# Two of layer 1's adaLN groups computed by VectorE in layer 0's second feed-forward product, TensorE summing over partitions only

## The chip, the cores and the metric

The kernel runs on one core of a Trainium2 chip. Its time is the device time of one launch in microseconds. The core has five engines with a queue each, which meet only through semaphores: TensorE (PE, matmuls; its weight loads are listed as PEld), VectorE (DVE), ScalarE (ACT), GpSimd (POOL) and SyncE (SP, which issues nearly all DMAs).

## The reference

One denoising step of a two-layer hybrid backbone with 512 latent tokens and 128 prompt tokens (640 columns together), D = 1024. What matters here is the modulation, its uses, and the feed-forward product in whose time the change computes it:

```python
def trunk_layer(x, cond, p, ...):
    mod = (jax.nn.silu(cond) @ p['w_ada'] + p['b_ada'])[:, None, :]
    sh1, sc1, gt1, sh2, sc2, gt2 = jnp.split(mod, 6, axis=-1)
    h = rmsnorm(x, p['g_pre_mix']) * (1.0 + sc1) + sh1
    ... = _split(h @ p['w_in'], IN_SIZES)          # gated DeltaNet, HGRN2 and attention mixers
    x = x + gt1 * rmsnorm(mix @ p['w_out'], p['g_post_mix'])
    h = rmsnorm(x, p['g_pre_ffn']) * (1.0 + sc2) + sh2
    ff_a, ff_b = jnp.split(h @ p['w_ffn_in'], 2, axis=-1)
    x = x + gt2 * rmsnorm((jax.nn.silu(ff_a) * ff_b) @ p['w_ffn_out'], p['g_post_ffn'])
```

There are two conditioning vectors (latent and prompt), so `mod` is a product of two rows of 1024 with a 1024 x 6144 matrix in each layer.

## The kernel before

All activations lie with features on partitions and tokens on columns, in two halves of 320 columns. A matrix product keeps fp32 precision with three matmuls of split numbers (high x high, high x low, low x high): a weight block arrives by DMA in a `raw` buffer (L592), ScalarE writes its high part `wh` (L582), VectorE the rest `wl` (L583), and TensorE multiplies (L606). The adaLN matrix is taken in unsplit fp32, by matmuls of only 32 rows of output (L276, `silu_c` is silu of the conditioning, `cst` and `onet` hold constants).

`w_ada` is stored as three groups per layer, each 8 blocks of 128 rows by 4 pieces of 512 columns, 256 KB per block and piece. Group 0 gives the shift and gain of the input norm, groups 1 and 2 ("2 and 3" if one counts from one) the rest. `ada` is a generator: each step issues one load and one matmul (L275, L276), four pieces going to four column quarters of the array; at the end of a group ScalarE copies the sum (L282), four transposes turn it onto partitions (L285), and VectorE adds the biases (L290). `GR` says which groups a layer computes for itself: groups 1 and 2, in its input stage, in `gdn` right after the raw part of the first gated DeltaNet pair (`fill(100)`). There they lie in program order among the w_in product and the DeltaNet's convolutions and chunk terms (L743, L787, L846). Group 0 of layer 1 is computed in layer 0's feed-forward stage, a few steps at a time.

Layer 0's second feed-forward product (`ffo`) multiplies 22 blocks of activations, `fs`, each a high and a low part, with w_ffo. The first four output tiles take both halves at once; then tiles 4 to 7 of the first half, then those of the second. A finished tile is copied from PSUM by ScalarE (L1449) into a block `ys`, and its square is added to a statistic by ScalarE (L389) and VectorE (L391). The last `fs` blocks are split (L583) just before the product.

The order of instructions on each engine is fixed when the kernel is built: a scheduler goes by priorities (weights first), by free buffers and by the code's order. SBUF blocks come in tags: `h` (8 blocks), `r` (12), `w0` and `w1` (7 each); PSUM tags have two buffers each. An engine runs its instructions in that order and stands still where one has to wait.

Of the kernel before, what the change touches and what calls it, by code (L numbers as in the profile page):

```python
# [12 lines left out]
ALU = mybir.AluOpType  # L13
AX = mybir.AxisListType

L = 2
D = 1024
KD = 8
# [14 lines left out]
def local(piece):  # L33
    a, b = HALVES[piece]
    return slice(a - BASE[piece], b - BASE[piece])
# [12 lines left out]
NSP, NFILL, NPACE = 6, 8, 8  # L48
AD0, AD1 = 7, 3
UTAGS = ("w1", "w1", "w1", "h", "h", "r", "r", "r")  # L50
SPRI = 5000
NKEEP = 6
GR = (1, 2), (1, 2)
MPRI = 8000
HPRI = 0
KPRI = 0
# [10 lines left out]
V_GPM, V_GOM, V_GPF, V_GOF, V_BADA = 0, 8, 16, 24, 32  # L67
# [97 lines left out]
class Builder:  # L165
# [40 lines left out]
    def setup(self):  # L206
# [52 lines left out]
            nc.vector.tensor_tensor(out=self.lb[:, l], in0=g[:, l], in1=g[:, 0], op=ALU.subtract)  # L259
        nc.vector.tensor_scalar(out=self.lb1, in0=self.lb, scalar1=-1.0, scalar2=1.0, op0=ALU.mult, op1=ALU.add)  # L260

    def ada(self, l, groups, tag, btag, depth):
        nc, I = self.nc, self.I
        ring = [self.blk([128, 2, 512], tag=btag) for _ in range(depth)]
        unit = 0
        if l not in self.mods:
            self.mods[l] = self.small("mods", [128, 48, 2], bufs=2)
        mods = self.mods[l]
        for ng in groups:
            acc = self.ps(tag=tag)  # L270
            for k in range(KD):
                for j in range(4):
                    raw = ring[unit // 2 % depth][:, unit % 2]
                    unit += 1
                    nc.sync.dma_start(out=raw, in_=I["w_ada"][l, ng, k, j])  # L275
                    nc.tensor.matmul(acc[32 * j:32 * j + 32, :], lhsT=self.sc[:, k, :], rhs=raw,  # L276
                                     start=(k == 0), stop=(k == KD - 1), tile_position=(0, 32 * j))
                    if j % 2 or k + 1 < KD:
                        yield
            row = ring[unit // 2 % depth][:, unit % 2]  # L280
            unit += 1
            nc.scalar.activation(row, acc, AF.Copy)  # L282
            tp = self.ps(tag=tag)
            for b in range(4):
                nc.tensor.transpose(tp[:, b * 128:(b + 1) * 128], row[:, b * 128:(b + 1) * 128], self.ident)  # L285
            tpv = tp.rearrange("p (b j r) -> p b j r", b=4, j=4)
            for b in range(4):
                mv = mods[:, ng * 16:(ng + 1) * 16].rearrange("p (j b) s -> p j b s", b=4)[:, :, b]
                bv = self.vec[:, l, V_BADA + ng * 16:V_BADA + (ng + 1) * 16].rearrange("p (j b) -> p j b", b=4)[:, :, b]
                nc.vector.tensor_tensor(out=mv, in0=tpv[:, b, :, 0:2],  # L290
                                        in1=bv.unsqueeze(2).to_broadcast([128, 4, 2]), op=ALU.add)
            self.ada_end(l, ng)
# [1028 lines left out]
    def layer(self, l, h):  # L1321
        nc, I = self.nc, self.I
# [7 lines left out]
                for n in pre:  # L1330
                    self.gemm_acc(pre[n], I["w_in"][l, n], hv, KD, k0)
        inp = lambda n, halves=(0, 1): pre.pop(n) if n in pre else self.gemm(I["w_in"][l, n], hv, KD, halves)
        filler = self.ada(l, GR[l], "c1", "w1", AD0)
        fill = lambda n: [next(filler, None) for _ in range(n)]
        rb = lambda shape: self.blk(shape, tag="r")
        r2 = rb([128, 2, NT])
# [62 lines left out]
        for s in range(2):  # L1399
            tag, bt = f"c{s}", ("w1", "r")[s]  # L1400
# [11 lines left out]
            h2[s] = self.norm_quads(ts, sx, m["G2"], m["sh2"], s, tag, bt)  # L1412
        fs = [self.blk([128, 2, NT], F32R, "w0") for n in range(NSP)]
        ffi = lambda n, halves: self.gemm(I["w_ffi"][l, n], lambda e, k, s: h2[s][k // 4][e][:, k % 4], KD, halves)
        filler = self.ada(l + 1, tuple(g for g in range(3) if g not in GR[l + 1]), "c0", "r", AD1) if l + 1 < L else iter(())
        for halves in ((0,), (1,)):
            for n in range(NSP):
                pa = ffi(2 * n, halves)
# [6 lines left out]
        last, us = None, []  # L1425
# [7 lines left out]
        last()  # L1433
        fill(100)
        self.retable()
        for u, tag in zip(us, ["w0"] * (7 - NSP) + ["r"] * 4 + ["w1"] * 7 + ["r"] * 4):
            fs.append(self.blk([128, 2, NT], F32R, tag))
            self.split(fs[-1][:, 0], fs[-1][:, 1], u)
        ys = [self.wide("r") for s in range(2)]
# [3 lines left out]
        hn, xs = [None, None], {}  # L1443
        for pieces, ns in (((0, 1), range(4)),) + tuple(((q,), range(4, KD)) for q in (0, 1)):
            for n in ns:
                ps = ffo(n, pieces)
                for q in pieces:
                    s, sl = min(q, 1), local(q)
                    nc.scalar.activation(ys[s](n)[:, sl], ps[q], AF.Copy)  # L1449
                    self.stat_add(sy[s], ys[s](n)[:, sl], n, sl)  # L1450
            if len(pieces) == 2:
                continue
            q = pieces[0]
            s = min(q, 1)
            tag, bt = f"c{s}", ("h", "w0")[s]
            if s not in xs:
                xs[s] = self.x_load(self.xd[2 * l], s, bt)
            ts, x = xs[s]
            if nl is None:
                self.post_norm(x, ys[s], sy[s], m["P2"], q, tag)  # L1460
                a, b = HALVES[q]
                for g in range(2):
                    nc.sync.dma_start(out=self.O["yT"][:, 4 * g:4 * g + 4, a:b], in_=ts[g][:, :, local(q)])
            else:
                sx = self.stat(bt)
                self.post_norm(x, ys[s], sy[s], m["P2"], q, tag, sx)
                self.x_store(self.xd[2 * l + 1], s, ts)
                hn[s] = self.norm_mod(x, sx, nl["G1"], nl["sh1"], s, tag)
# [110 lines left out]
```

## Time and profile before

| | us |
|---|---|
| median of 3 runs | 2006.32 (2006.19 to 2007.88) |
| the profiled execution | 2005.87 |
| span of the profiled execution | 2004.1 |
| TensorE busy in it | 1938.8 |
| VectorE busy | 1296.2 |
| ScalarE busy | 1001.2 |

The profile covers one execution. Its span goes from the first to the last instruction, 1.8 us less than that execution's own time. All times of rows are from the start of the span. A busy time is the union of an engine's instructions; "x4" is a count of records, and a row of a timeline that has a count merges neighbours of one kind. For a matmul the profile writes two records to each fp32 matmul.

### The profile page before, as it was taken

What the parts mean: (1) busy time and instruction counts of PE and PEld (TensorE: products, weight loads), DVE (VectorE), ACT (ScalarE), POOL (GpSimd) and SP (SyncE); (2) the same over time, 40 slices, a digit from 0 to 9 for tenths busy, and PEclk for the clock granted to TensorE, in tenths of its full rate; (3) what the DMA queues carried; (4) which work ended last, traced back from release to release, by engine and by line L of the source; (5) the groups of instructions that cost most, each with busy time, mean ns of one, the idle gap of its engine ahead of it and who ended that gap; (6) DMA issues with size and microseconds to landing.
All of it is one profiled execution on the core that took longest, in us unless ns stands there. A gap on an engine that the chain in (4) does not pass through costs nothing. (4 is left out here: it accounts for less than half of the span.)

```text
span 2004.1 us, 39984 instructions
## 1 busy us (share of the span) xinstructions
PE 1938.8 (97%) x15696; PEld 1724.3 (86%) x15696; DVE 1296.2 (65%) x2834; ACT 1001.2 (50%) x2088; POOL 16.4 (1%) x64
## 2 busy tenths in 40 slices
PE   5999999999999999999999999999999999999997
PEld 2747888888999979999997497888899999999996
DVE  5627567685588657762586386678756977777245
ACT  3514253754676435552465251547457855555243
POOL 0000000000000000000000000000000000000000
PEclk9999999999999999999999999999999999999998
DMA  8643211110554452232585532112016542223344
GB/s 300 205 163 89 59 47 32 58 32 3 188 181 152 137 165 85 89 114 79 155 271 163 184 97 57 31 40 59 5 59 210 163 123 89 87 88 88 101 137 140
DMA packets 157997, 226.57 MB, mean 113 GB/s; under 512 B 39280, under 2 KB 66032, under 8 KB 157808
## 3 DMA queue, kind: packets, MB, share of 16 engines
q1 hardware_dynamic: 157168, 222.70, 36.1%
q8 instruction: 123, 2.02, 0.4%
q0 software_dynamic: 640, 1.31, 0.3%
q14 instruction: 66, 0.54, 0.1%
HBM read 209.99 MB, written 12.65 MB: 111 GB/s over the span
## 5 line engine op out<-in xcount | busy, mean ns | idle before, releaser
L582 ACT ACTIVATE wh<-raw 128x512 fp32r<-128x512 f32 (+2 forms) x634 | 391.4, 617 | 591.9 <-PE g L606 410.1
L583 DVE TENSOR_TENSOR wl<-raw,wh 128x512 fp32r<-128x512 f32 (+1 forms) x610 | 408.8, 672 | 376.0 <-ACT wh L582 336.0
L606 PE MATMUL g<-h,wh 128*128 128x320 f32 x2448 | 541.3, 318 | 1.6 <-DVE su L1297 0.7
L606 PEld LDWEIGHTS g<-h,wh 128*128 128x128 f32 x2448 | 397.4, 188 | 50.2 <-issue 28.8
L606 PE MATMUL g<-h,wl 128*128 128x320 f32 x1224 | 337.1, 316 | 0.5 <-DVE wl L583 0.5
L606 PE MATMUL g<-w,wh 128*128 128x320 f32 x1152 | 242.5, 311 | 5.5 <-ACT r L1405 5.5
L606 PEld LDWEIGHTS g<-h,wl 128*128 128x128 f32 x1224 | 215.9, 188 | 21.4 <-issue 15.6
L606 PEld LDWEIGHTS g<-w,wh 128*128 128x128 f32 x1152 | 188.8, 189 | 6.3 <-ACT r L1405 6.0
L606 PE MATMUL g<-r,wh 128*128 128x320 f32 x768 | 162.9, 310 | 0.0
L606 PE MATMUL g<-w,wl 128*128 128x320 f32 x480 | 131.0, 310 | 0.0
L513 PE MATMUL g<-h,wh 128*128 128x320 f32 x768 | 129.1, 310 | 0.0
L606 PEld LDWEIGHTS g<-r,wh 128*128 128x128 f32 x768 | 125.9, 188 | 0.5
L513 PEld LDWEIGHTS g<-h,wh 128*128 128x128 f32 x768 | 116.3, 188 | 3.6 <-issue 3.4
L507 DVE TENSOR_TENSOR raw<-raw,raw 128x512 f32<-128x512 f32 x128 | 88.0, 688 | 2.2
L606 PEld LDWEIGHTS g<-w,wl 128*128 128x128 f32 x480 | 86.0, 189 | 0.2
L513 PE MATMUL g<-w,wh 128*128 128x320 f32 x512 | 85.9, 310 | 0.0
L513 PE MATMUL g<-r,wh 128*128 128x320 f32 x512 | 85.5, 309 | 0.0
L276 PE MATMUL m<-w,silu_c 128*32 128x512 f32 x256 | 83.4, 603 | 0.2 <-DMA w<-in_w_ada_dram 0.2
L513 PEld LDWEIGHTS g<-w,wh 128*128 128x128 f32 x512 | 77.6, 188 | 3.4 <-ACT r L525 3.4
L606 PE MATMUL g<-r,wl 128*128 128x320 f32 x288 | 78.6, 309 | 0.0
L513 PEld LDWEIGHTS g<-r,wh 128*128 128x128 f32 x512 | 77.7, 188 | 0.0
L513 PE MATMUL g<-h,wl 128*128 128x320 f32 x384 | 71.9, 309 | 0.0
(373 smaller groups left out, 3030.2 us busy)
## 6 DMA issues: line engine op xcount, KB each, us to landing
raw<-in_w_ffi_dram SPq DMA_DIRECT2D x224, 256.0 KB
w<-in_w_ada_dram SPq DMA_DIRECT2D x160, 256.0 KB
raw<-in_w_ffo_dram SPq DMA_DIRECT2D x120, 256.0 KB
raw<-in_w_in_dram SPq DMA_DIRECT2D x106, 256.0 KB
raw<-in_w_out_dram SPq DMA_DIRECT2D x64, 256.0 KB
r<-in_w_ada_dram SPq DMA_DIRECT2D x32, 256.0 KB
r<-in_xT_dram SPq DMA_DIRECT2D x6, 640.0 KB
xd<-w SPq DMA_DIRECT2D x6, 640.0 KB
```

Of the source, the lines that this page charges most:

```text
L276: nc.tensor.matmul(acc[32 * j:32 * j + 32, :], lhsT=self.sc[:, k, :], rhs=raw, start=(k == 0), stop=(k == KD - 1), tile_position=(0, 32 * j))
L507: nc.vector.tensor_tensor(out=o, in0=a, in1=b, op=ALU.add)
L513: nc.tensor.matmul(ps, lhsT=w[e][:, k], rhs=a[f][:, k], start=first and i == 0, stop=i == 11, skip_group_check=not first)
L582: self.nc.scalar.activation(hi, src, AF.Copy)
L583: self.nc.vector.tensor_tensor(out=lo, in0=src, in1=hi.bitcast(F32), op=ALU.subtract)
L606: self.nc.tensor.matmul(ps[h], lhsT=w[:, k], rhs=rhs(e, kk, h), start=(kk == 0 and i == 0), stop=(kk == nk - 1 and i == 2))
```

## The change

Layer 1 no longer computes groups 1 and 2 for itself (`GR[1]` is empty). A new generator, `ada_vec`, does it in layer 0's second feed-forward product. A unit is one piece of 512 columns of one group, and there are eight. VectorE multiplies each of the eight 128x512 blocks with the conditioning (one number per partition) and adds them up in `acc`, for both conditionings: 2 `tensor_scalar_mul` and 14 `scalar_tensor_tensor`. Then TensorE sums over the partitions: eight matmuls with a single column of ones (`onet`), into one PSUM tile, and VectorE adds the biases. The loads are 512 KB each, four to a unit, into a ring of two blocks of tag `r`; `acc` is a third. Two units are placed ahead of each of the first four output tiles. To make room for a block, the last `fs` block moves from tag `r` to `h`. Group 0 of layer 1 is computed where it was.

```diff
-GR = (1, 2), (1, 2)
+GR = ((1, 2), ())
+PE_NEXT, VEC_NEXT = (0,), (1, 2)
+VRING = 2
...
+    def ada_vec(self, l, groups, tag, btag):
+        nc, I = self.nc, self.I
+        mods = self.modulation(l)
+        acc = self.blk([128, 2, 512], tag=btag)
+        ring = [self.blk([128, 2, 512], tag=btag) for _ in range(VRING)]
+        for ng in groups:
+            for j in range(4):
+                for k in range(KD):
+                    raw = ring[k // 2 % VRING]
+                    if k % 2 == 0:
+                        nc.sync.dma_start(out=raw, in_=I["w_ada"][l, ng, k:k + 2, j].rearrange("k p n -> p k n"))
+                    for s in range(2):
+                        c = self.sc[:, k, s:s + 1]
+                        if k == 0:
+                            nc.vector.tensor_scalar_mul(acc[:, s], raw[:, 0], c)
+                        else:
+                            nc.vector.scalar_tensor_tensor(out=acc[:, s], in0=raw[:, k % 2], scalar=c, in1=acc[:, s],
+                                                           op0=ALU.mult, op1=ALU.add)
+                tp = self.ps((128, 4, 2), tag)
+                for s in range(2):
+                    for b in range(4):
+                        nc.tensor.matmul(tp[:, b, s:s + 1], lhsT=acc[:, s, b * 128:(b + 1) * 128], rhs=self.onet, start=True, stop=True)
+                q = ng * 16 + j * 4
+                bv = self.vec[:, l, V_BADA + q:V_BADA + q + 4]
+                nc.vector.tensor_tensor(out=mods[:, q:q + 4], in0=tp, in1=bv.unsqueeze(2).to_broadcast([128, 4, 2]), op=ALU.add)
+                yield
+            self.ada_end(l, ng)
...
-        filler = self.ada(l, GR[l], "c1", "w1", AD0)
+        filler = self.ada(l, GR[l], "c1", "w1", AD0) if GR[l] else iter(())
...
-        filler = self.ada(l + 1, tuple(g for g in range(3) if g not in GR[l + 1]), "c0", "r", AD1) if l + 1 < L else iter(())
+        filler = self.ada(l + 1, PE_NEXT, "c0", "r", AD1) if l + 1 < L else iter(())
...
-        for u, tag in zip(us, ["w0"] * (7 - NSP) + ["r"] * 4 + ["w1"] * 7 + ["r"] * 4):
+        filler = self.ada_vec(l + 1, VEC_NEXT, "c0", "r") if l + 1 < L else iter(())
+        for u, tag in zip(us, ["w0"] * (7 - NSP) + ["r"] * 4 + ["w1"] * 7 + ["r"] * 3 + ["h"]):
...
         for pieces, ns in (((0, 1), range(4)),) + tuple(((q,), range(4, KD)) for q in (0, 1)):
             for n in ns:
+                if len(pieces) == 2:
+                    fill(2)
                 ps = ffo(n, pieces)
...
             if len(pieces) == 2:
+                fill(100)
                 continue
```

In the changed program lines have moved: L582, L583, L606 and L1449 are L615, L616, L639 and L1485. A row names a line, an operation, the block written and those read, with numbers that tell blocks apart; `r_9622` is `acc`, `r_9623` and `r_9624` are the ring, `m` and `g` are PSUM tiles, and the brackets name what the instruction waits for.

VectorE at the start of the second feed-forward product, in the changed program. Ahead is the last split of the activations; in the program before, only weight splits and statistics follow it.

```order
L616 TENSOR_TENSOR h_9613<-r_9272,h_9613 128x640 [waits DVE_49]
L283 TENSOR_SCALAR r_9622<-r_9623,silu_c 128x512 [waits DMAHW5_49]
L283 TENSOR_SCALAR r_9622<-r_9623,silu_c 128x512
L285 SCALAR_TENSOR_TENSOR r_9622<-r_9623,silu_c,r_9622 128x512 [waits DVE_49] x2
L616 TENSOR_TENSOR wl_9839<-raw_9837,wh_9838 128x256 [waits DMAHW0_49,PE_49,Activation_49]
L688 TENSOR_SCALAR ga_n_11912<-ga_n_11912 128x4
L285 SCALAR_TENSOR_TENSOR r_9622<-r_9624,silu_c,r_9622 128x512 [waits DMAHW0_49,DVE_49]
L285 SCALAR_TENSOR_TENSOR r_9622<-r_9624,silu_c,r_9622 128x512 [waits DVE_49] x3
L616 TENSOR_TENSOR wl_9923<-raw_9921,wh_9922 128x512 [waits DMAHW1_49,PE_49,Activation_49]
```

Each block of the ring gives four operations on VectorE, and a weight split follows about every fourth of them; 112 rows of L285 and 16 of L283 stand in this stretch, with 34 weight splits between.

TensorE where the third one-half tile of the first half begins (tile 6), in the program before and then in the changed one.

```order
L606 MATMUL g_10430<-r_9613,wh_10522 128x320 x2
L606 MATMUL g_10430<-r_9613,wl_10523 128x320
L606 MATMUL g_10536<-w_886_6295,wh_10538 128x320 [waits Activation_49]
L606 MATMUL g_10536<-w_886_6295,wh_10538 128x320
L606 MATMUL g_10536<-w_886_6295,wl_10539 128x320 [waits DVE_49]
```

```order
L639 MATMUL g_10680<-h_9613,wl_10773 128x320
L290 MATMUL m_10353<-onet,r_9622 128x1 [waits DVE_49,PE_49]
L290 MATMUL m_10353<-onet,r_9622 128x1 x3
L290 MATMUL m_10353<-onet,r_9622 128x1 [waits DVE_49]
L290 MATMUL m_10353<-onet,r_9622 128x1 x3
L639 MATMUL g_10786<-w_886_6295,wh_10788 128x320 [waits Activation_49]
L639 MATMUL g_10786<-w_886_6295,wh_10788 128x320
L639 MATMUL g_10786<-w_886_6295,wl_10789 128x320
L639 MATMUL g_10786<-w_887_6296,wh_10788 128x320 x2
L639 MATMUL g_10786<-w_887_6296,wl_10789 128x320
L639 MATMUL g_10786<-w_888_6297,wh_10788 128x320 x2
L290 MATMUL m_10383<-onet,r_9622 128x1 [waits DVE_49,PE_49]
```

The narrow matmuls of unit 7 (`m_10353`) now stand at the end of tile 5, and those of unit 8 (`m_10383`) after the first eight matmuls of tile 6; the six units before stand earlier, spread over the tiles 0 to 5.

ScalarE at its copy of the first one-half tile (tile 4), before and then changed.

```order
L1449 ACTIVATE r_9617<-g_10324 128x320 [waits PE_49]
L389 ACTIVATE h_9620<-r_9617 128x320 [waits Activation_49]
L582 ACTIVATE wh_10486<-raw_10485 128x512 [waits DMAHW6_49,DVE_49,PE_49]
```

```order
L615 ACTIVATE wh_10824<-raw_10823 128x512 [waits DMAHW4_49,DVE_49,PE_49]
L1485 ACTIVATE r_9617<-g_10574 128x320 [waits DMAHW1_49,DVE_49]
L1485 ACTIVATE r_9617<-g_10680 128x320 [waits PE_49]
L422 ACTIVATE h_9620<-r_9617 128x320 [waits Activation_49] x2
L615 ACTIVATE wh_10842<-raw_10841 128x512 [waits DMAHW5_49,PE_49]
```

The copy waited for TensorE alone; now it waits for a load and for VectorE, since its target `r_9617` takes the place of a ring block, and it stands next to the copy of tile 5.

TensorE in layer 1's input stage, before and then changed, where the DeltaNet's triangular terms of the first pair begin.

```order
L606 MATMUL g_12707<-h_11309,wl_12740 128x320
L606 MATMUL g_12706<-h_10795,wh_12739 128x320
L276 MATMUL m_12089<-w_1840_12008,silu_c 32x512 [waits DMAHW1_49]
L606 MATMUL g_12707<-h_11309,wh_12739 128x320
L606 MATMUL g_12706<-h_10797,wh_12739 128x320
L787 MATMUL m_12230<-r_11687 64x128 [waits DVE_49,PE_49]
L787 MATMUL m_12230<-r_11687 64x128 x2
L276 MATMUL m_12089<-w_1840_12008,silu_c 32x512 [waits DMAHW2_49]
L787 MATMUL m_12230<-r_11687 64x128
```

```order
L639 MATMUL g_12870<-h_11558,wl_12873 128x320
L639 MATMUL g_12869<-h_11044,wh_12872 128x320
L820 MATMUL m_12290<-r_11937 64x128 [waits DVE_49,Activation_49]
L820 MATMUL m_12290<-r_11937 64x128 x7
L820 MATMUL m_12303<-r_11937 64x128 [waits Activation_49]
L820 MATMUL m_12303<-r_11937 64x128 x7
L639 MATMUL g_12870<-h_11558,wh_12872 128x320
```

The adaLN matmuls (L276) are gone from this stage, and w_in's matmuls (L606, now L639) stand next to the DeltaNet's (L787, now L820).

## Rows read from the trace of the kernel before

**Rows 1.** The page's table of engines: busy us, share of the span, instructions.

```profile
PE 1938.8 (97%) x15696; PEld 1724.3 (86%) x15696; DVE 1296.2 (65%) x2834; ACT 1001.2 (50%) x2088; POOL 16.4 (1%) x64
```

**Rows 2.** Stretches of 10 us, second feed-forward product: length, engines' busy us, clock, DMA.

```profile
core 0: us, PE busy (x) PEld busy (x) DVE busy (x) ACT busy (x) POOL busy (x), PEclk, DMA share, GB/s
...
880.00:890.00 10.00, 10.00 (x70) 10.00 (x69) 2.12 (x5) 1.68 (x3) 0.00 (x0) 1.00 0.24 67
890.00:900.00 10.00, 10.00 (x70) 10.00 (x69) 2.10 (x4) 2.91 (x6) 0.00 (x0) 1.00 0.66 213
...
940.00:950.00 10.00, 10.00 (x70) 10.00 (x69) 2.51 (x4) 2.88 (x7) 0.00 (x0) 1.00 0.27 73
950.00:960.00 10.00, 10.00 (x70) 10.00 (x69) 4.56 (x8) 4.52 (x9) 0.00 (x0) 1.00 0.46 129
```

**Rows 3.** Timeline of ScalarE: copies of finished tiles (start us, us, what).

```profile
949.04 0.75 ACT L1449 ACTIVATE r<-g 128x320 f32<-128x320 f32 x2
...
958.87 0.42 ACT L1449 ACTIVATE r<-g 128x320 f32<-128x320 f32 x1
...
968.55 0.42 ACT L1449 ACTIVATE r<-g 128x320 f32<-128x320 f32 x1
```

**Rows 4.** Timeline of VectorE: the last split of the activations.

```profile
879.42 0.82 DVE L583 TENSOR_TENSOR r<-r,r 128x640 fp32r<-128x640 f32 x1
```

**Rows 5.** Timeline of TensorE, layer 1's input stage.

```profile
1094.76 4.67 PE L276 MATMUL m<-w,silu_c 128*32 128x512 f32 x30
...
1101.03 2.03 PE L276 MATMUL m<-w,silu_c 128*32 128x512 f32 x4
...
1124.36 1.05 PE L276 MATMUL m<-w,silu_c 128*32 128x512 f32 x2
...
1153.24 1.05 PE L276 MATMUL m<-w,silu_c 128*32 128x512 f32 x2
...
1155.04 0.60 PE L285 MATMUL m<-cst,w 128*128 128x128 f32 x4
...
1167.65 1.24 PE L743 MATMUL m<-w,cst 128*128 128x512 f32 x4
```

**Rows 6.** Timeline of TensorE's weight loads around one adaLN group; brackets: idle before, releaser.

```profile
1124.36 0.14 PEld L276 LDWEIGHTS m<-w,silu_c 128*32 128x32 f32 x2 [0.19 <-issue]
1125.33 0.30 PEld L606 LDWEIGHTS g<-h,wh 128*128 128x128 f32 x2 [0.84 <-issue]
```

**Rows 7.** Stretches of 10 us from 1090 to 1170, and their sum.

```profile
1100.00:1110.00 10.00, 10.00 (x45) 4.74 (x43) 2.35 (x9) 4.40 (x11) 0.68 (x2) 1.00 1.00 370
...
1160.00:1170.00 10.00, 10.00 (x67) 9.52 (x66) 8.43 (x15) 4.00 (x10) 0.00 (x0) 1.00 0.36 96
sum 80.00, PE 80.00 PEld 46.45 DVE 38.54 ACT 26.60 POOL 2.26; mean PE 10.00 PEld 5.81 DVE 4.82 ACT 3.33 POOL 0.28
```

**Rows 8.** Two more stretches of 10 us, ahead of and behind those.

```profile
1020.00:1030.00 10.00, 10.00 (x69) 9.76 (x67) 6.82 (x13) 6.49 (x15) 0.34 (x6) 1.00 0.93 310
...
1170.00:1180.00 10.00, 9.88 (x60) 8.76 (x59) 9.72 (x28) 9.44 (x19) 0.00 (x0) 1.00 0.33 105
```

**Rows 9.** VectorE's instruction groups, shapes apart: busy us, mean ns, idle before.

```profile
L583 DVE TENSOR_TENSOR wl<-raw,wh 128x512 fp32r<-128x512 f32 x566 | 388.6, 688 | 337.9 <-ACT wh L582 298.2 <-PE g L606 16.3 <-PE g L513 11.1
L690 DVE SCALAR_TENSOR_TENSOR w<-w,vec,w 128x642 f32<-128x642 f32 x48 | 42.5, 885 | 1.1
...
L1243 DVE TENSOR_SCALAR h<-h,smax 128x640 f32<-128x640 f32 x32 | 17.6, 551 | 0.7
...
L575 DVE SCALAR_TENSOR_TENSOR r<-r,P,h 128x320 f32<-128x320 f32 x16 | 8.2, 545 | 1.7 <-ACT h L357 1.7
```

**Rows 10.** Timeline of VectorE: two neighbouring multiply-adds.

```profile
1001.53 1.01 DVE L575 SCALAR_TENSOR_TENSOR r<-r,P,h 128x320 f32<-128x320 f32 x2
```

**Rows 11.** Timeline of SyncE's queue and TensorE: an adaLN load and the matmul that waits.

```profile
708.43 0.33 SPq L275 DMA_DIRECT2D r<-in_w_ada_dram  x1
...
711.50 1.04 PE L276 MATMUL m<-r,silu_c 128*32 128x512 f32 x2 [0.29 <-DMA r<-in_w_ada_dram]
```

**Rows 12.** Stretches of 2 us around a wait of TensorE in layer 1's mixers.

```profile
1458.00:1460.00 2.00, 0.93 (x17) 0.60 (x12) 0.29 (x1) 0.60 (x1) 0.00 (x0) 0.97 0.00 0
1460.00:1462.00 2.00, 2.00 (x9) 1.75 (x10) 1.20 (x5) 1.28 (x5) 0.00 (x0) 0.50 0.00 0
1462.00:1464.00 2.00, 2.00 (x11) 1.79 (x10) 1.25 (x6) 1.49 (x5) 0.00 (x0) 0.67 0.03 8
```

More of the change, by code (lines that the diff above doesn't have):

```diff
@@ L260, in setup, with modulation @@
         nc.vector.tensor_scalar(out=self.lb1, in0=self.lb, scalar1=-1.0, scalar2=1.0, op0=ALU.mult, op1=ALU.add)
+    def modulation(self, l):
+        if l not in self.mods:
+            self.mods[l] = self.small("mods", [128, 48, 2], bufs=2)
+        return self.mods[l]
+    def ada_vec(self, l, groups, tag, btag):
[25 more added lines that the diff above has]
+            self.ada_end(l, ng)
     def ada(self, l, groups, tag, btag, depth):
@@ L265, in ada @@
         unit = 0
-        if l not in self.mods:
-            self.mods[l] = self.small("mods", [128, 48, 2], bufs=2)
-        mods = self.mods[l]
+        mods = self.modulation(l)
         for ng in groups:
```

## The prediction

> **What bounds the kernel now.** I read the page's table of engines first: TensorE is busy 97% of the span, the other engines far less [rows 1], so a microsecond taken from TensorE counts only where nothing else ends last, and one added to another engine counts only where TensorE then waits. So I read the two stages that the change touches, one after the other.
>
> *Where the work goes: layer 0's second feed-forward product.* The table by 10 us stretches shows TensorE full there, and VectorE at 2.1 to 2.5 of 10 us through the tiles that compute both halves, 4.6 of 10 after [rows 2]. ScalarE's copies of finished tiles give the pace: two-half tiles come out until 949.04, then one tile every 9.68 us (958.87, 968.55) [rows 3]; that is 66 matmuls (22 blocks of the inner dimension, 3 products) at 0.147 us. The window from VectorE's last split of the activations, 879.42 + 0.82 [rows 4], to the copy at 949.04 is 69 us long.
>
> *Where the work comes from: layer 1's input stage.* The timeline of TensorE shows a first block of adaLN matmuls of 4.67 us, then single groups of 1.04 to 1.05 us, strewn among the w_in product until 1153.24, and two groups of transposes of 0.60 us [rows 5]. Around one of them, the weight loads show that the next ordinary load starts 0.97 us after the group's own, which had itself waited 0.19 us [rows 6]: a group takes 1.16 us out of the stream.
>
> **Part 1, layer 1: what is removed.** In the timeline from 1094.76 to 1155.04 I count the block (4.60 us to the next matmul), one double group (1.95 + 0.19) and 25 single ones (25 x 1.16 = 29.0), and two transposes (1.2): 36.9 us. Six more groups lie at 1050.9 to 1063, where TensorE waits for the norm of the input anyway; I give them 0 to 1.5 us. So the gain is at most 38.4 us. What takes some of it back: once TensorE no longer fills the stage, VectorE and ScalarE must bring the same steps of the gated DeltaNet in less time. Between 1090 and 1170, VectorE is busy 38.54 and ScalarE 26.60 of 80 us, but VectorE is at 8.43 in the last 10 us of it [rows 7] and at 9.72 in the 10 us behind [rows 8]. With 36.9 us out, the 80 us shrink to 43, less room than VectorE has work unless it runs at 0.9 of busy. In 1020 to 1030, where splits and norms compete in the same way, it reached 6.82 of 10 [rows 8]. At that share 38.5 us of work takes 56 us: gain 24. I take 31, the middle of 24 and 38.4, since TensorE does have other w_in matmuls to run while the chain waits and VectorE's queue is not in every window that poor. The loads of these two groups (64 of 256 KB) leave a stretch whose DMA share reached 1.00 [rows 7]; that is inside the 0 to 1.5.
>
> **Part 2, layer 0: VectorE's added work.** Per unit of 512 columns of one group: 2 multiplications and 14 multiply-adds of 128x512, and there are 8 units: 16 and 112. The trace has no multiply-add of 128x512 with a scalar from a column; 128x320 takes 545 ns and 128x642 takes 885 [rows 9], so 128x512 lies at 746. A multiplication of 128x640 takes 551 [rows 9]; by its slope I take 484 for 512. Two neighbouring multiply-adds of 128x320 take 1.01 us together, not 1.09 [rows 10]: the next starts 0.08 early. So the pitches are 0.666 and 0.404, and the sum is 112 x 0.666 + 16 x 0.404 = 81.1 us (91.3 by full durations). Between them, in the order of the changed program, stand 28 splits of 128x512 (688 ns in [rows 9], pitch 0.61), 6 of 128x256, 4 additions of statistics and 8 of biases: 22.3 us (25.4 by durations). So VectorE's stretch is 103.4 us: begun at 880.2, it ends at 983.6 if it never waits, at 996.9 if nothing overlaps. **It does not fit into the 69 us.**
>
> It will wait, too. At each of the 7 changes of unit the first multiplication overwrites the sum that TensorE has still to read: some 1.3 us for signal, eight narrow matmuls and signal back, 9 us in all. And the ring has two blocks: a block is loaded again only when it has been used up. A 256 KB load of the same tensor took 3.07 us from issue to the matmul that waited for it [rows 11]; the other 256 KB of a 512 KB load add 0.7 us at the 370 GB/s of [rows 7], so 3.8. Meanwhile VectorE uses the other block up (4 x 0.666 = 2.7 us, and 0.7 of splits): it waits 0 to 0.4 us at each of 32 blocks, in the mean 0.3, or 10 us. End of the last unit: 983.6 + 9 + 10 = **1003** (993 without waiting for loads, 1015 at the upper ends).
>
> **Who waits for that.** TensorE runs in program order, and the narrow matmuls of the units stand in its row: five units among the two-half tiles, the sixth in the second one-half tile, the seventh at its end, the eighth after only 8 matmuls of the third. So the last two units are not covered: VectorE needs some 15 us for a unit (123 us for 8), and TensorE has only 48 matmuls (7 us) between the sixth and the seventh and 8 (1.2 us) between the seventh and the eighth. A second tie points the same way: the copy of the first one-half tile writes a block that the ring had, so ScalarE waits there for the last unit's third block, and the third one-half tile for ScalarE, since two PSUM buffers serve these tiles. In the trace of before, the eighth matmul of the third one-half tile starts at about 968.55 + 8 x 0.147 = 969.7 [rows 3]. Now it goes on at 1003 + 0.9 (the last four narrow matmuls): 34.2 us later; by the bounds 24 to 46. The 128 records of narrow matmuls, about 0.12 us each by four transposes in 0.60 us [rows 5], run inside that wait. After TensorE had stood still for half of a 2 us stretch, the granted clock in the next two stretches was 0.50 and 0.67 of full speed, so at the lower of its two levels (1.2 of 2.4 GHz) for a time [rows 12]; that cost 0.50 x 2 + 0.33 x 2 = 1.7 us there. Two waits here are longer: I add 2.5 us, 0 to 3.4 as bounds. Part 2: **+36.7**, from 24 to 49.
>
> **Sum.** 2005.87 (the profiled execution) + 36.7 - 31 = 2011.6; the median of the runs shown is 0.45 above the profiled one: **2012**.
>
> **Rivals.**
> *A, VectorE keeps up better (the other side).* Place: the second feed-forward product. If the ring's loads come in time and the changes of unit cost half of what I took, the last unit ends at 988 and TensorE loses 988 + 0.9 - 969.7 = 19, and if VectorE is no bound in layer 1, 37 comes back: 2005.9 + 19 + 1.7 - 37 = 1989; with one of the two only, 1996 to 2006. For it: the raw loads leave the queues at 0.24 to 0.66 share in this stretch [rows 2]. Against it: the 103.4 us hold no wait at all. It decides from an end of the last unit before about 996 at a full gain. Chance 0.22.
> *B, layer 1 gives back only 24,* because VectorE becomes the bound from 1130 on: 2005.9 + 36.7 - 24 = 2019. For it: 9.72 of 10 in [rows 8]. Against: TensorE has other tiles to run. Chance 0.15.
> *C, the ring is the bound:* a period of 3.8 us or more per block, since the issuing queue also holds weight loads that wait for their buffers in order. 32 x 0.8 us of waiting instead of 10 in all: end at 1018, +15: 2027. Chance 0.09.
> *D, nothing overlaps on VectorE:* each multiply-add waits by semaphore for the one two places ahead, on the same half of the sum. If that wait uses up the 0.08, the stretch ends at 996.9 + 9, and the loads are then hidden behind the longer steps: 1006, so 2005.9 + 36.2 + 2.5 - 31 = 2014, 2 us above the forecast. Against it: [rows 10], 1.01 us for two independent steps of 545 ns. Chance 0.04. The Trainium skill's page "VectorE: DVE Perf Modes", section "The DRAIN you can't avoid", says that the next VectorE operation does not start before the pipeline of the one ahead is empty, which speaks against chains of small steps like these; by that rule the durations would hold in full and D would be the case, and for independent steps [rows 10] do not agree with it.
>
> **How the numbers follow.** The forecast has the remaining 0.50, with a range of its own of 2003 to 2021 (end of the last unit 996 to 1009, gain 27 to 35). About 0.2% (4 us) is what a measurement of this kernel can tell from no change: 2002.3 and 2010.3 are the limits. Faster: A 0.20, the forecast's lower end 0.05: 0.25. Within: A 0.02, the forecast 0.16, B 0.02: 0.20. Slower: the rest, 0.55. Range for 8 in 10: at 1996 about 0.11 is left out below (the better part of A), at 2027 about 0.09 above.
>
> **What would show it.** Right: in the second feed-forward product VectorE near 9 of 10 us from 880 to about 1000; TensorE with waits for VectorE at the narrow matmuls of units 7 and 8 of about 5 to 20 us in all, or for ScalarE's copy ahead of the third one-half tile; this tile's copy about 35 us late; the granted clock down once or twice behind these waits. The distance from there to the L743 group of the second pair (1167.65 in [rows 5]) about 25 to 30 us shorter than before, and some 31 at the end of the stage. Wrong, if multiply-adds of 128x512 take much under 0.67 us apiece, if TensorE waits only a few microseconds there, or if VectorE is not full between 1090 and 1190 (shifted) and the stage shrinks by 37 all the same.

## The result, and the profile after

The changed kernel takes 2016.87 us (median of 4 runs, 2014.74 to 2022.63) where the kernel before, measured beside it, takes 2006.26. The ratio is 1.0056, with a 95% interval of 1.0044 to 1.0068: **11 us slower** (9 to 14). The forecast was 2012, in a range of 1996 to 2027.

The span of the profiled execution is 2020.8 us. It was the longest of the four, and some 4 us of that arose ahead of the changed place, as ScalarE's copies of finished tiles show. First those of the kernel before that [rows 3] leave out (the first tile, and tiles 6 and 7), then the same copies of the kernel after (start, us, what; in brackets the idle time before and who ended it).

```profile
890.96 0.75 ACT L1449 ACTIVATE r<-g 128x320 f32<-128x320 f32 x2
...
978.23 0.42 ACT L1449 ACTIVATE r<-g 128x320 f32<-128x320 f32 x1
987.90 0.42 ACT L1449 ACTIVATE r<-g 128x320 f32<-128x320 f32 x1
```

```profile
895.19 0.75 ACT L1485 ACTIVATE r<-g 128x320 f32<-128x320 f32 x2
922.28 0.75 ACT L1485 ACTIVATE r<-g 128x320 f32<-128x320 f32 x2
943.66 0.75 ACT L1485 ACTIVATE r<-g 128x320 f32<-128x320 f32 x2
967.76 0.75 ACT L1485 ACTIVATE r<-g 128x320 f32<-128x320 f32 x2
1010.20 0.77 ACT L1485 ACTIVATE r<-g 128x320 f32<-128x320 f32 x2 [20.25 <-DVE r L285]
1028.34 0.42 ACT L1485 ACTIVATE r<-g 128x320 f32<-128x320 f32 x1
```

The first tile is 4.2 us late. After it, tile by tile, the product falls behind: tile 3 by 19, and tile 6 by 50.1 (1028.34 against 978.23). So layer 0's product costs 46 us in this execution. Between tiles 3 and 4 ScalarE stands for 20.25 us and waits for VectorE: its next copy writes a block that the ring still holds.

The stretches of 10 us (columns as in [rows 2]) show the same on all engines.

```profile
880.00:890.00 10.00, 10.00 (x70) 10.00 (x69) 8.74 (x16) 2.58 (x6) 0.00 (x0) 1.00 0.60 194
...
900.00:910.00 10.00, 10.00 (x50) 10.00 (x50) 4.99 (x9) 1.26 (x2) 0.00 (x0) 0.67 0.69 233
...
950.00:960.00 10.00, 10.00 (x69) 10.00 (x70) 9.16 (x16) 1.69 (x3) 0.00 (x0) 1.00 0.61 203
...
990.00:1000.00 10.00, 1.52 (x8) 1.55 (x8) 6.87 (x12) 0.00 (x0) 0.00 (x0) 0.60 0.54 174
1000.00:1010.00 10.00, 2.02 (x10) 1.94 (x10) 7.60 (x13) 0.00 (x0) 0.00 (x0) 0.50 0.49 158
1010.00:1020.00 10.00, 9.31 (x38) 9.32 (x39) 4.56 (x10) 2.11 (x5) 0.00 (x0) 0.50 0.03 4
```

VectorE, at 2.1 to 2.5 of 10 in [rows 2], is now at 8 to 10 in most stretches. The exception is 900 to 910, with 4.99. There TensorE's granted clock was 0.50 from 900 to 906, behind a wait of 0.82 us at 897, so the mean of the ten microseconds is 0.67 and TensorE lost 3.3 us; in the middle of it VectorE stood 3.66 us for a weight split, whose first half ScalarE could write only when TensorE had freed a buffer:

```profile
907.63 0.63 ACT L615 ACTIVATE wh<-raw 128x512 fp32r<-128x512 f32 x1 [5.09 <-PE g L639]
908.30 0.69 DVE L616 TENSOR_TENSOR wl<-raw,wh 128x512 fp32r<-128x512 f32 x1 [3.66 <-ACT wh L615]
```

From 990 to 1010 TensorE works 1.5 to 2 us of each 10, and from 1010 to 1020 it works again, but at a granted clock of 0.50, its lower level (1.2 of 2.4 GHz). TensorE's timeline has the two waits that make this hole:

```profile
998.48 3.54 PE L290 MATMUL m<-onet,r 128*128 128x1 f32 x16 [9.06 <-DVE r L285]
1010.69 0.90 PE L639 MATMUL g<-w,wh 128*128 128x320 f32 x2 [8.66 <-ACT r L1485]
```

The first is unit 7's narrow matmuls waiting for VectorE, the second is tile 6 waiting for ScalarE's copy. VectorE's own waits from 884 to 1012 (us in total, times, longest) and its two new groups (busy us, mean ns):

```profile
DVE mods L293 <- PE m L290: 8.5, 7, 1.6
DVE r L285 <- DMA r<-in_w_ada_dram: 6.1, 7, 2.1
DVE wl L616 <- ACT wh L615: 5.2, 5, 3.7
DVE r L283 <- PE m L290: 3.0, 4, 1.4
...
L285 DVE SCALAR_TENSOR_TENSOR r<-r,silu_c,r 128x512 f32<-128x512 f32 x112 | 77.8, 746 | 6.1 <-DMA r<-in_w_ada_dram 6.1
L283 DVE TENSOR_SCALAR r<-r,silu_c 128x512 f32<-128x512 f32 x16 | 7.5, 482 | 3.0 <-PE m L290 3.0
```

In layer 1 the time comes back. The row that answers to L846 at 1205.08 in the timeline of before is L879 here, first before and then after:

```profile
1205.08 1.09 PE L846 MATMUL m<-w,w 64*64 64x64 f32 x30
```

```profile
1221.15 1.03 PE L879 MATMUL m<-w,w 64*64 64x64 f32 x28
```

It is 16.1 us late, as the end of the span is (16.7), where tile 6 was 50.1 late: layer 1's input stage gives back 34 us. 46 lost, 34 returned, 12 net, beside the 11 of the ratio.

### The profile page after: what moved, and what is told of

Read it like the earlier page. It is cut to its first block, busy times and chain, and to the rows that moved or that the text cites. A ratio compares the mean times of both kernels' runs of the same rounds, so it can differ in the third digit from the quotient of the medians.

```text
span 2020.8 us, 40048 instructions
## 1 busy us (share of the span) xinstructions
PE 1931.9 (96%) x15688; PEld 1746.5 (86%) x15688; DVE 1375.6 (68%) x2962; ACT 1000.2 (49%) x2086; POOL 16.1 (1%) x64
## 5 line engine op out<-in xcount | busy, mean ns | idle before, releaser
L615 ACT ACTIVATE wh<-raw 128x512 fp32r<-128x512 f32 (+2 forms) x634 | 391.4, 618 | 614.2 <-PE g L639 425.5
L616 DVE TENSOR_TENSOR wl<-raw,wh 128x512 fp32r<-128x512 f32 (+1 forms) x610 | 408.3, 671 | 313.7 <-ACT wh L615 267.5
L639 PE MATMUL g<-h,wh 128*128 128x320 f32 x2512 | 554.3, 318 | 3.2 <-ACT h L482 1.2
L639 PEld LDWEIGHTS g<-h,wh 128*128 128x128 f32 x2512 | 409.0, 188 | 39.2 <-issue 18.7
L639 PE MATMUL g<-h,wl 128*128 128x320 f32 x1256 | 345.4, 316 | 0.5 <-DVE wl L616 0.5
L639 PE MATMUL g<-w,wh 128*128 128x320 f32 x1152 | 249.5, 317 | 14.2 <-ACT r L1485 8.7
L639 PEld LDWEIGHTS g<-h,wl 128*128 128x128 f32 x1256 | 222.2, 188 | 15.5 <-issue 9.7
L639 PEld LDWEIGHTS g<-w,wh 128*128 128x128 f32 x1152 | 193.6, 193 | 15.0 <-ACT r L1485 8.7
L639 PE MATMUL g<-r,wh 128*128 128x320 f32 x704 | 151.9, 313 | 0.0
L639 PE MATMUL g<-w,wl 128*128 128x320 f32 x480 | 133.9, 316 | 0.0
L546 PE MATMUL g<-h,wh 128*128 128x320 f32 x768 | 129.1, 310 | 0.0
L546 PEld LDWEIGHTS g<-h,wh 128*128 128x128 f32 x768 | 116.3, 188 | 3.6 <-issue 3.4
L639 PEld LDWEIGHTS g<-r,wh 128*128 128x128 f32 x704 | 117.0, 190 | 0.5
L639 PEld LDWEIGHTS g<-w,wl 128*128 128x128 f32 x480 | 88.7, 194 | 0.2
L546 PE MATMUL g<-w,wh 128*128 128x320 f32 x512 | 85.9, 310 | 0.0
L546 PE MATMUL g<-r,wh 128*128 128x320 f32 x512 | 85.5, 309 | 0.0
L285 DVE SCALAR_TENSOR_TENSOR r<-r,silu_c,r 128x512 f32<-128x512 f32 x112 | 77.8, 746 | 6.1 <-DMA r<-in_w_ada_dram 6.1
L546 PEld LDWEIGHTS g<-w,wh 128*128 128x128 f32 x512 | 77.5, 188 | 3.4 <-ACT r L558 3.4
L546 PEld LDWEIGHTS g<-r,wh 128*128 128x128 f32 x512 | 77.7, 188 | 0.0
L546 PE MATMUL g<-h,wl 128*128 128x320 f32 x384 | 71.9, 309 | 0.0
L639 PE MATMUL g<-r,wl 128*128 128x320 f32 x256 | 70.8, 312 | 0.0
```

Of the source, the lines that this page charges most:

```text
L285: nc.vector.scalar_tensor_tensor(out=acc[:, s], in0=raw[:, k % 2], scalar=c, in1=acc[:, s], op0=ALU.mult, op1=ALU.add)
L546: nc.tensor.matmul(ps, lhsT=w[e][:, k], rhs=a[f][:, k], start=first and i == 0, stop=i == 11, skip_group_check=not first)
L615: self.nc.scalar.activation(hi, src, AF.Copy)
L616: self.nc.vector.tensor_tensor(out=lo, in0=src, in1=hi.bitcast(F32), op=ALU.subtract)
L639: self.nc.tensor.matmul(ps[h], lhsT=w[:, k], rhs=rhs(e, kk, h), start=(kk == 0 and i == 0), stop=(kk == nk - 1 and i == 2))
```

## The experiments

Each kernel below is the changed kernel with an edit, unless it says otherwise; ratios are to the kernel before, on the same chip, with their 95% intervals, and differences in microseconds are taken from the ratio at 2006.

### What each part costs by itself

Neither part (groups 1 and 2 of layer 1 set to zero):

```diff
+    def ada_none(self, l, groups):
+        self.nc.vector.memset(self.modulation(l)[:, 16:48], 0.0)
...
-        filler = self.ada_vec(l + 1, VEC_NEXT, "c0", "r") if l + 1 < L else iter(())
+        filler = self.ada_none(l + 1, VEC_NEXT) if l + 1 < L else iter(())
...
```

> Leaves out: layer 1's adaLN groups 1 and 2 are computed nowhere (their values are set to zero). It shows what layer 1's input stage gives back by itself. Theory (TensorE bounds that stage but for a few microseconds): the two traces of before and after part by 33.5 us there, so 33 us less than before, about 1973 us. Rival 1 (VectorE becomes the bound as soon as TensorE's filling is gone; part of the 33.5 is only there because layer 0's long wait of TensorE gave the other engines a head start): 20 to 25 less, 1981 to 1986. Rival 2 (the adaLN matmuls were mostly hidden): within 10 of before.

Measured: 1972.85 us, ratio 0.983 (0.9814 to 0.9847): 34 less. Layer 1 gives back 34 us also where TensorE had no long wait ahead of it, so rival 1 falls, and the 36.9 to 38.4 us of TensorE's time that were removed come back but for 3 to 4. Where those stay, the stretches of this kernel show: TensorE is no longer full, VectorE is.

```profile
1120.00:1130.00 10.00, 10.00 (x70) 10.00 (x69) 9.82 (x15) 6.62 (x14) 0.00 (x0) 1.00 0.31 75
1130.00:1140.00 10.00, 8.77 (x58) 8.06 (x56) 9.86 (x23) 6.48 (x11) 0.00 (x0) 1.00 0.36 98
1140.00:1150.00 10.00, 8.96 (x63) 6.21 (x64) 9.65 (x28) 6.53 (x17) 1.74 (x3) 1.00 0.20 62
```

TensorE's own waits there, 2.1 us in all, end with instructions of ScalarE; that VectorE, full at the time, is behind them is likely, but no run shows it.

Both parts (the groups are computed twice, VectorE's result is dropped):

```diff
-GR = ((1, 2), ())
+GR = ((1, 2), (1, 2))
...
-        mods = self.modulation(l)
+        spare = self.small("spare", [128, 4, 2])
...
```

> Leaves nothing of the reference out but does groups 1 and 2 of layer 1 twice: by VectorE in layer 0's second feed-forward product (that result is dropped) and, as before, by TensorE in layer 1. It shows what the added part costs by itself. Theory (VectorE ends late, TensorE waits for it, and the two parts add): the ratio of the change is 1.0056, +11 us; with 33 from layer 1 that makes the cost 42 to 46, so about 2050 us. Rival (the cost is less, and the change is slow because layer 1 gives little back): 2030 to 2036.

Measured: 2053.49 us, ratio 1.0233 (1.0218 to 1.0248): 47 more. The two parts, -34 and +47, add up to +13, and the change measures +11 (9 to 14): within the intervals they do not act on each other, and the prediction could rightly be made as a sum.

### Which limit sets layer 0's cost

The ring is not reloaded (all units work on the first two blocks):

```diff
-                    if k % 2 == 0:
+                    if k % 2 == 0 and ng == groups[0] and j == 0 and k < 2 * VRING:
```

> Leaves out the reloading of the ring: only the first two loads of w_ada are issued, all eight units work on these two blocks, so the values are not the reference's; VectorE's and TensorE's instructions are those of the change. Theory (VectorE's own 104 us of work is the bound): the 6 us that VectorE waits for loads in the trace of the change go, the last unit ends at 1006 instead of 1013, and the time is 5 to 8 us less than the change, about 2010 us. Rival (the two-block ring and SyncE's queue are what keeps VectorE from being in time): 15 us or more less than the change, under 2002 us.

Measured: 2005.82 us, ratio 0.9996 (0.9986 to 1.0007): 12 less than the change, more than the theory gave and less than the rival. VectorE's waits in the answering stretch, 880 to 996, show why it is more than the 6.1 us of waiting for loads: the waits at changes of unit and for ScalarE's halves of the splits have shrunk as well (here 5.7 + 3.4 and 2.9, after 8.5 + 3.0 and 5.2).

```profile
DVE mods L293 <- PE m L290: 5.7, 7, 1.6
DVE r L283 <- PE m L290: 3.4, 5, 1.3
DVE wl L616 <- ACT wh L615: 2.9, 5, 0.9
DVE r L285 <- DMA r<-in_w_ada_dram: 1.2, 1, 1.2
```

Part of the 12 is not settled by this run: with no loads the scheduler also put some narrow matmuls elsewhere in TensorE's row.

One block in another tag:

```diff
-        acc = self.blk([128, 2, 512], tag=btag)
+        acc = self.blk([128, 2, 512], tag="h")
```

> The change with one word altered: the block in which VectorE adds up has tag h instead of r. The copy of the first one-half tile then needs no block of the ring (only the second half's copies do, some 40 us later), and the scheduler puts unit 7's narrow matmuls into the third one-half tile and unit 8's to the end of the fourth. Theory A (what makes TensorE stand 18 us is that tie of SBUF blocks: VectorE's late end is then covered by two more tiles): layer 0 loses 20 to 26 instead of 46 (16 of it narrow matmuls), time 1994 to 2001. Theory B (VectorE's end alone decides; without the tie TensorE waits for unit 8 just as long): within 5 of the change, 2012 to 2017.

Measured: 1995.86 us, ratio 0.9945 (0.9926 to 0.9963): 11 less than before and **22 less than the change, by one word**. Theory A's time holds. ScalarE's copies of this kernel, tiles 3 to 7, TensorE's waits from 880 to 1040, and the first narrow matmuls of units 7 and 8:

```profile
968.71 0.75 ACT L1485 ACTIVATE r<-g 128x320 f32<-128x320 f32 x2
978.53 0.42 ACT L1485 ACTIVATE r<-g 128x320 f32<-128x320 f32 x1
990.44 0.42 ACT L1485 ACTIVATE r<-g 128x320 f32<-128x320 f32 x1
1001.93 0.42 ACT L1485 ACTIVATE r<-g 128x320 f32<-128x320 f32 x1
1011.61 0.42 ACT L1485 ACTIVATE r<-g 128x320 f32<-128x320 f32 x1
...
PE m L290 <- DVE h L285: 3.2, 5, 1.1
...
997.62 0.98 PE L290 MATMUL m<-onet,h 128*128 128x1 f32 x8
...
1016.29 1.02 PE L290 MATMUL m<-onet,h 128*128 128x1 f32 x8 [0.82 <-DVE h L285]
```

Tile 6 is at 1001.93, 26 us earlier than after the change, though tile 3 is at the same place (968.71 and 967.76). The wait of 20.25 us on ScalarE is gone, and of TensorE's 19.7 us of waiting 3.2 are left. Units 7 and 8 end no earlier on VectorE; but their narrow matmuls now stand in tile 6 and behind tile 7 (997.62 and 1016.29), and TensorE computes these tiles meanwhile.

The one word changes two things at once: ScalarE's copy no longer waits for a ring block, and the narrow matmuls of units 7 and 8 have later places in TensorE's row. The run does not part them. As the change's trace reads, each held tile 6 back to about the same time by itself: the copy let it begin at 1010.69, and where unit 8's narrow matmuls stood, eight matmuls into tile 6, TensorE would have had to wait for VectorE's end at 1012.8 with or without the copy.

The cost of layer 0's product that remains is 22 us: tiles 6 and 7 are 23.7 late, some 4.5 of that come from ahead of the product in this execution, and unit 8 adds 3 behind tile 7. It is nearly all TensorE's: eight units with two groups of eight records of narrow matmuls, 0.95 to 1.02 us each, make 15.6 us; 3.2 are waits; and two 10 us stretches with a granted clock of 0.83 cost 1.7 us apiece.

Idle matmuls where TensorE stood:

```diff
                 ps = ffo(n, pieces)
+                if pieces == (0,) and n == 5 and l + 1 < L:
+                    dummy = self.ps((128, 320), "c1")
+                    for _ in range(108):
+                        nc.tensor.matmul(dummy, lhsT=fs[0][:, 0, 0:128], rhs=fs[0][:, 0, 0:320], start=True, stop=True)
```

> The change with 108 idle matmuls of 128x320 (their result is not used) where TensorE stands in the change: 54 ahead of unit 7's narrow matmuls, 54 behind them, 7.9 us each time against waits of 9.1 and 8.7 us. They add nothing to the path if the waits are as the trace shows. Theory (the low clock that follows the wait is a cost of its own: in the change's trace 0.50 for 30.7 us, of which TensorE works some 12 us): the granted clock stays at 1.00 through the wait and the time is 5 to 7 us less than the change, about 2011. Rival (the low clock costs nothing, since VectorE's end decides until unit 8): the same as the change, 2015 to 2018, or a few us more where the fill is longer than a wait.

Measured: 2008.82 us, ratio 1.0011 (1.0001 to 1.0022): 9 less than the change, with 108 matmuls more. The stretch behind the waits in this kernel has the full clock, where the change has 0.50:

```profile
990.00:1000.00 10.00, 9.23 (x68) 8.99 (x67) 6.63 (x14) 0.00 (x0) 0.00 (x0) 1.00 0.51 167
1000.00:1010.00 10.00, 8.32 (x59) 8.06 (x57) 8.37 (x13) 2.12 (x5) 0.00 (x0) 1.00 0.35 107
1010.00:1020.00 10.00, 10.00 (x73) 10.00 (x74) 4.57 (x10) 3.57 (x7) 0.00 (x0) 1.00 0.34 92
```

VectorE does not end earlier here. ScalarE's copies of tile 0, of tiles 4 and 5, and of tile 6:

```profile
891.02 0.74 ACT L1489 ACTIVATE r<-g 128x320 f32<-128x320 f32 x2
...
1006.62 0.77 ACT L1489 ACTIVATE r<-g 128x320 f32<-128x320 f32 x2 [19.29 <-DVE r L285]
1019.25 0.42 ACT L1489 ACTIVATE r<-g 128x320 f32<-128x320 f32 x1
```

Tile 0 is on time, and the copy of tiles 4 and 5 is where the change has it without its 4.2 us of lateness (1006.0). From there to tile 6 it is 12.6 us, in the change 18.1; tile 6 is 41.0 us late instead of 45.9. So the low clock is a cost of its own, beside the wait that it follows, of about 5 us here. The rest of the 9 arises in layer 1, and no run shows from what.

### Half of the work, and the same half on TensorE

Only group 1 on VectorE, one unit ahead of each two-half tile:

```diff
-GR = ((1, 2), ())
-PE_NEXT, VEC_NEXT = (0,), (1, 2)
+GR = ((1, 2), (2,))
+PE_NEXT, VEC_NEXT = (0,), (1,)
...
-                    fill(2)
+                    fill(1)
```

> Only group 1 (four units) goes to VectorE, one unit ahead of each two-half tile; group 2 stays with TensorE in layer 1. Theory (the loss is a queue that VectorE cannot empty in time, so it falls on the last units): the fourth unit ends at about 945 us, before its place in TensorE's row is reached, so layer 0 loses only the narrow matmuls (4 x 1.9 us) and 1 to 4 us of waits and clock, and layer 1 returns half of 33: 2006 - 16.5 + 10 = 1997 to 2002 us. Rival (every unit costs alike, through the narrow matmuls, the port or the loads): half of the change's +11, about 2012 us.

Measured: 1994.04 us, ratio 0.9939 (0.9924 to 0.9954): 12 less than before, and 3 less than the theory's lower end. The cost in layer 0 is at the upper end of the expectation, some 11.5 us (tile 6 is 12.7 late, the first tile 1.1): narrow matmuls, two waits of TensorE for VectorE of 1.9 us together, and a stretch at a clock of 0.83. What was expected wrongly is the return: tile 6 is copied 12.7 us later than in the kernel before (978.23), L879 starts 11.9 us earlier (1205.08), so half of the groups gives back 25 us and not half of 34. The adaLN matmuls that stay in layer 1 show why (timelines of ScalarE and TensorE in this kernel):

```profile
990.90 0.42 ACT L1485 ACTIVATE r<-g 128x320 f32<-128x320 f32 x1
...
1107.43 3.63 PE L309 MATMUL m<-w,silu_c 128*32 128x512 f32 x28
1111.24 1.05 PE L309 MATMUL m<-w,silu_c 128*32 128x512 f32 x2 [0.18 <-DMA w<-in_w_ada_dram]
1113.89 1.85 PE L309 MATMUL m<-w,silu_c 128*32 128x512 f32 x4
...
1193.15 1.15 PE L879 MATMUL m<-w,w 64*64 64x64 f32 x32
```

The group that is left runs at the start of the stage, where 28 records follow one another in 3.63 us; in the kernel before, many of the matmuls come in separate groups of two records at 1.05 us apiece [rows 5]. Counted in the two traces, TensorE's adaLN matmuls in this stage make up 33 separate groups before and 10 here, 39 and 15 us. The dear half is the one that comes second.

The same half on TensorE, in layer 0's first feed-forward product:

```diff
-GR = ((1, 2), ())
-PE_NEXT, VEC_NEXT = (0,), (1, 2)
+GR = ((1, 2), (2,))
+PE_NEXT, VEC_NEXT = (0, 1), ()
...
-        filler = self.ada_vec(l + 1, VEC_NEXT, "c0", "r") if l + 1 < L else iter(())
+        filler = iter(())
```

> VectorE has no adaLN work: layer 1's group 1 is computed by TensorE in layer 0's first feed-forward product, behind group 0 and in the same way, group 2 stays in layer 1. The one group takes TensorE 64 records there, 16 us by the 16.2 us that group 0's 64 records take. Theory (it is the place that counts in layer 1, where the group costs 25 us; on VectorE it costs 11.5 us of layer 0, on TensorE 16 to 18): 2006.3 - 25 + 17 = 1996 to 2000 us, 3 to 6 above the half on VectorE. Rival (in layer 0 the adaLN matmuls come singly as in layer 1 and cost 25 there too): 2004 to 2008, no gain.

Measured: 1995.4 us, ratio 0.9939 (0.9924 to 0.9954), the same as with VectorE and just below the expectation's lower end of 1996. VectorE is not needed for that gain: it is the place in layer 1 that was dear.

### Fewer, larger groups on TensorE

From the row "x28 in 3.63 us" comes a version that moves nothing. The kernel before, with two pieces of w_ada in one load:

```diff
-                    nc.sync.dma_start(out=raw, in_=I["w_ada"][l, ng, k, j])
+                    if j % 2 == 0:
+                        nc.sync.dma_start(out=ring[(unit - 1) // 2 % depth], in_=I["w_ada"][l, ng, k, j:j + 2].rearrange("j p n -> p j n"))
...
-                    if j % 2 or k + 1 < KD:
+                    if j % 2:
                         yield
...
-            unit += 1
+            unit += 2
```

> The kernel before, VectorE without adaLN work, groups 1 and 2 with TensorE in layer 1 as ever; only the loads of w_ada behind the first layer's start come 512 KB at a time (two pieces of 512 columns), so that the two matmuls of a pair, on different columns of the array, become ready together. Theory (what the adaLN costs TensorE in a full stage is the number of separate groups, 1.16 us each, whether a group holds two records or eight: rows of before show 1.05 us for x2, x4 and x8): about half as many groups, 10 to 14 us less in layer 1 and 4 to 7 less for group 0 in layer 0, so 1986 to 1992 us. Rival (the cost goes by matmul): no change, 2003 to 2009.

Measured: 1983.69 us, ratio 0.9895 (0.9878 to 0.9911): 21 less than before, more than expected, for a reason the expectation left out: layer 0 computes two groups for itself in its own input stage, in the same strewn way, and instruction by instruction, of the 24 us by which the profiled execution is shorter, some 14 are there; layer 1 gives about 10. In the feed-forward stage, where 4 to 7 were expected, there is less than one microsecond. The number of separate groups fits: counted in the traces, it falls from 47 to 34 in layer 0's input stage and from 33 to 25 in layer 1's, which at the prediction's 1.16 us apiece makes 15 and 9 us, and goes from 12 to 14 in the feed-forward stage. The loads are also twice as large here, but waiting for them is not what was saved: in layer 0's input stage TensorE waits 0.2 us for w_ada before and 2.3 us with pairs.

Paired loads (the edit just shown), with group 1 on TensorE in layer 0:

```diff
-GR = ((1, 2), ())
-PE_NEXT, VEC_NEXT = (0,), (1, 2)
+GR = ((1, 2), (2,))
+PE_NEXT, VEC_NEXT = (0, 1), ()
...
```

> As the run with group 1 in TensorE's row of layer 0 (1995 us), and paired loads. Theory: the two groups in layer 0 cost some 9 us each instead of 16 and group 2 in layer 1 a little less, so 1978 to 1984 us, the fastest so far. Rival (cost by matmul): 1995, no change.

Measured: 1985.15 us, ratio 0.9897 (0.9882 to 0.9912), no better than pairs alone: the expectation failed. In layer 0's first feed-forward product pairs are worse than single loads. Unpaired, a burst of 12 records takes 1.91 us there (first row, from the kernel with group 1 on TensorE); paired, nearly each group of four stands alone (the others, from this kernel); for the two adaLN groups there are 29 separate ones instead of 20. Why they part is not shown.

```profile
704.44 1.91 PE L309 MATMUL m<-r,silu_c 128*32 128x512 f32 x12
```

```profile
689.22 1.05 PE L310 MATMUL m<-r,silu_c 128*32 128x512 f32 x4
690.99 1.05 PE L310 MATMUL m<-r,silu_c 128*32 128x512 f32 x4
694.51 1.05 PE L310 MATMUL m<-r,silu_c 128*32 128x512 f32 x4
```

Paired loads, with group 1 on VectorE and its sum in a block of tag `h`:

```diff
-GR = ((1, 2), ())
-PE_NEXT, VEC_NEXT = (0,), (1, 2)
+GR = ((1, 2), (2,))
+PE_NEXT, VEC_NEXT = (0,), (1,)
...
-        acc = self.blk([128, 2, 512], tag=btag)
+        acc = self.blk([128, 2, 512], tag="h")
...
...
-                    fill(2)
+                    fill(1)
```

> Group 1 on VectorE in layer 0's second feed-forward product (four units, its sum in a block of tag h), group 2 with TensorE in layer 1, paired loads for what TensorE computes. Theory: the half on VectorE gave 1994; pairs take 4 to 7 us from group 0 in layer 0 and 0 to 3 from group 2: 1985 to 1990 us, above the run with group 1 on TensorE and paired, since four units cost 11.5 us in layer 0 and a paired group 9. Rival (VectorE is the better place): below that run.

Measured: 1972.9 us, ratio 0.9838 (0.9815 to 0.986): **32 less than before, the fastest** version that computes everything. The rival holds: beside pairs, the group is worth 11 us on VectorE and nothing on TensorE in layer 0, where pairs made the place dear.

## Why the prediction was right

The sign was right, and so was the mechanism in the main: VectorE ends late, TensorE waits for it and comes back at the low clock, and layer 1 returns less than that costs. The size was too small: +6 forecast, +11 measured (9 to 14). Part of its nearness is luck, since layer 0 cost 10 us more than forecast and layer 1 gave 3 more back. By its own steps:

- **VectorE's price and its sum.** Right. 746 ns were interpolated for the multiply-add and 746 were measured; 484 and 482 for the multiplication. Rows of x4 in 2.74 us give a pitch of (2.74 - 0.746) / 3 = 0.665, against 0.666. The stretch began at 884.39, 880.1 without the 4.2 us of lateness (forecast 880.2), and VectorE was busy for 104.4 us of it (forecast 103.4). So rival D, full durations, falls, though each step waits by semaphore for the one two places ahead. (In D's sum the wait should have been 1006 + 0.9 - 969.7 = 37.2, not 36.2.)
- **VectorE's waits: the first term that was mis-sized.** Forecast 9 + 10 us, measured 24.0: 8.5 + 3.0 at changes of unit (9 forecast), 6.1 for loads (10), and 5.2 that I did not have at all, weight splits that wait for ScalarE's half, which waits for TensorE to free a buffer; the other 1.2 are small gaps. In a queue that runs in order, the splits of the product itself hold up the added work. 3.66 of the 5.2 fall into TensorE's stretch at half clock from 900 to 906. They are not due to it alone: in the run with idle matmuls, where this stretch has the full clock, the waits for splits are 6.3 us, the longest 2.2. The last unit ended at 1012.8, or 1008.6 without the lateness: 5.6 after the forecast of 1003.
- **The clock: the second.** I added 0.9 for the last narrow matmuls and 2.5 for the clock. From VectorE's end (1012.8) to tile 6 (1028.34) there are 15.5 us, where before there were 8.5 from the eighth matmul (969.7) to the copy at 978.23: 7.0 instead of 3.4. The clock was down not for two stretches of a few microseconds, as in [rows 12], but from about 992, through the rest of the hole and for about 12 us of work behind it; at half speed that is 6 us, and the run with idle matmuls had tile 6 about 5 us earlier. The fall at 900, behind a wait of only 0.82 us, was not foreseen either.
- **Layer 0 in all:** 36.7 forecast, 46 in this trace and 47 by the run with both parts; inside the bounds of 24 to 49.
- **Who waits.** Both waits came, 9.06 us at unit 7's narrow matmuls and 8.66 us for ScalarE's copy ahead of tile 6. What the prediction did not see is that both change with the tag of one block. I took the units' places in TensorE's row as given and the block as "a second tie". The run with the block in tag `h` shows that one tag decides over tie and places together: with it tiles 6 and 7 run while VectorE finishes, and 22 of the 47 us go. How much of that is the tie and how much the places is open. VectorE's late end is then nearly free, and what is left is mainly the narrow matmuls, which I had let vanish inside the wait.
- **Layer 1.** 31 forecast as the middle of 24 and 38.4; measured 34. Rival B (24) falls. VectorE did become full, at 9.8 of 10, but for 30 us only, and 3 to 4 us were lost there rather than 14. My low end used the share of one stretch, 6.82 of 10, as if it were a limit; the stretch just ahead of it in the trace of before, 1010 to 1020, already had VectorE at 10.00, and the runs show it at 9.65 to 9.86.
- **Rival A** did not occur, and the point from which I let it decide, 996 for the end of the last unit, was too late: in the run without reloading VectorE is done at 996, and the time is that of the kernel before, where the rival's sum with 34 us back gives 2001 (2005.9 + 27.3 + 1.7 - 34). Tile 6 is 32.4 us late there instead of the sum's 29. **Rival C** falls with 6.1 us of waits for loads.

## What to carry to other kernels

The late end of work moved to an idle engine is free only as long as everything that waits for it lies behind other work; look not only at the consumer's place in the row, but at who inherits the buffers. Before moving small operations off the engine that bounds, look at what they cost where they are: here pairs of loads saved 21 us and the move, at its best without them, 12. And count the time after a long stall as well as the stall: here TensorE came back at the lower clock, which cost about 5 us.

## What the runs showed of the hardware

- A group of 32-column matmuls of 128x512 takes TensorE 1.04 to 1.06 us in nearly all cases, whether it holds 2, 4 or 8 records, and 28 in one run take 3.63; in this kernel the price goes by the number of separate groups.
- Eight records of the narrow fp32 matmul (128x1) take 0.95 to 1.02 us at full clock, hardly less than eight of the product's 128x320 records at 0.147 us apiece (1.18).
- After 18 us of waits within 22 us, the granted clock stayed at 0.50 for about 12 us of work; waits of 0.5 to 1.3 us in the same product were followed by 10 us stretches at 0.67 or 0.83, in some places and runs and not in others.
